# A decoder layer on one core: gathers and chunk loads change rooms, and the order of the sparse steps and of the gates' parts changes

## Chip, cores and metric

The kernel runs on one core of a Trainium2 chip. The time is what one execution takes on the device, in microseconds; each kernel is timed in several executions and the median is given. Engines are called as in the profile: PE (TensorE), DVE (VectorE), ACT (ScalarE), POOL (GpSimd) and SP (SyncE, which issues the large loads). POOL issues the gathers.

## The reference, cut to what matters

The layer has an attention and retention half and a feed-forward half that looks up experts by product keys. The change lies in the second half alone:

```python
PEER_HEADS, PEER_N_KEYS, PEER_TOPK = 8, 128, 16          # 16384 experts, D_MODEL = 2048, SEQ = 256

def peer_ffn(h, w_q, sub_keys, w_u, w_v):
    q = (hf @ w_q).reshape(T, PEER_HEADS, 2, PEER_QUERY_DIM // 2)
    s_half = jnp.einsum('thpd,hpkd->thpk', q, sub_keys)
    v_half, i_half = lax.top_k(s_half, K)
    ...
    top_s, pick = lax.top_k(cand_s, K)
    experts = jnp.take_along_axis(cand_i, pick, axis=-1)
    gates = jax.nn.softmax(top_s, axis=-1)
    ...
        a = jnp.einsum('cd,ced->ce', hc, w_u[ec])
        coef = gc * jax.nn.gelu(a)
        return jnp.einsum('ce,ced->cd', coef, w_v[ec])
```

Each of 256 tokens picks 16 experts in each of 8 heads, with a gate from a softmax over the 16. The result is the gated sum of the experts' v rows, each weighed with gelu of the token's product with the expert's u row. The sum is added to x with a gate and normalised once more.

## The kernel before

**Two ways through the experts.** For the first 192 tokens (`TD`) the kernel computes with all experts: it streams all of u and v, 128 chunks of 1 MB each, and masks by one-hot groups. For the last 64 tokens (`NS`) it gathers rows. The stream runs in four stages of 64 chunks (`HALF`), which fill the span from about 700 us on: `u_half` 0, `v_group` 0, `u_half` 1, `v_group` 1.

- `u_block` takes one u chunk: matmuls for 160 tokens (`TU`) into a PSUM block `psU`, ACT reads it through gelu into `X` (or into `ge`, which DVE multiplies into `X` where the mask is already there). There are two PSUM blocks.
- `v_group` takes one v chunk: ACT casts it to `whi`, DVE subtracts to `wlo` (`split`), ACT and DVE do the same for the coefficients (`cc`), and PE accumulates into eight PSUM banks `acc`: 12 matmuls with `whi`, 8 with `wlo`.
- `g_group` (160 tokens) and `m_group` (the 32 tokens from 160 to 191) make one-hot factors of indices and gates; `g_apply` multiplies them on PE (`pg`) and puts the mask into X. For the 32 tokens the products with u come not from the stream but from gathered rows.

**Sparse steps.** `plan` is a list of 160 steps. Each gathers 128 rows of 8 KB (1 MB) by an indirect DMA of POOL (`gather`) and then does one DVE instruction on them: 32 `m` steps (dots of the 32 tokens, L837, with `h2m`), 64 `u` steps (dots of the 64 tokens, L837, with `h2t`), 64 `v` steps (a chain that adds weighed v rows into `sp`, L843). When the last `m` step is done, `m_done` makes the weights `wm` that the four `m_group`s need; v_group 0 needs their columns of X. `sparse` is called once per chunk; `STEPS` says at which chunks of a stage a step is taken, and in v_group 1 the remaining steps are spread over the chunks. `fetch` keeps up to `most` gathers ahead of the steps.

**Rooms.** `places` says which tile a gather gets. In the u stages it is one of three rooms of `whi`; in v_group 0 one of two rooms of `more`; in v_group 1 a half of `x2` (in the trace `xT`, whose content is no longer needed). The chunk loads take their rooms in turn from the tags that `set_ring` names, always five rooms `raw`, and in the u stages `wlo` and `more` beside them.

**What sets the order.** The program is laid down in the order of the Python code, and a scheduler then fixes one static order of instructions for each engine by its own estimate of times. At run time every engine takes its instructions in that order, and waits where a room or an operand isn't ready.

**Gates.** While u_half 0 runs, a list `work` makes candidates, picks and gates for the two tiles of tokens, and then the groups; an item is taken when enough `budget` (2.4 per block) has gathered. `gates` is one item: DVE subtracts the maximum (`gt`), ACT takes Exp, DVE normalises, PE transposes, ACT casts the gates (`gat`), and for the second tile index and gate rows are copied to the sparse steps' tables.

## Time and profile before

| | us |
|---|---|
| median of 3 executions | 1982.16 (1979.97 to 1984.76) |
| profiled execution, its own time | 1989.1 |
| its span | 1987.3 |
| PE busy | 1825.5 (92%) |
| DVE busy | 1479.9 (74%) |
| ACT busy | 692.9 (35%) |
| POOL busy | 347.4 (17%) |

The stages end at about 1000.5, 1336.7, 1629.1 and 1931.5 us. How to read it: with PE at 92%, what is left lies in the places where PE waits. The slices of the page and stretches of 50 us show where; the timeline then gives the instruction that PE waited for, and what that one waited for. An engine's row stands in its static order, so an instruction that waits holds up all that stands behind it on its engine.

### The profile page before, as it was taken

The page shows a single profiled execution, that of the slowest core. Times are in us where ns is not written, and L with a number is a line of the kernel's source. Part 1 is how long each engine was busy: PE and PEld are TensorE (multiplying, and loading weights), DVE is VectorE, ACT ScalarE, POOL GpSimd, SP SyncE. Part 2 cuts the span into 40 slices and gives each one's busy share as a digit, 9 for nine tenths or more (in the row PEclk, how much of TensorE's full clock was granted, in tenths as well). Part 3 has the DMA queues.
Part 4 walks back from the last instruction along what each step waited for, and adds up shares of the span by engine and source line. Part 5 has one row for each costly group of instructions (what it writes and reads, how often), then busy time and mean ns, then how long its engine had stood idle before and what let it go on. Part 6 is the DMA issues. An engine that isn't in the chain of part 4 may idle for free.

```text
span 1987.3 us, 28481 instructions
## 1 busy us (share of the span) xinstructions
PE 1825.5 (92%) x11302; PEld 1594.7 (80%) x11302; DVE 1479.9 (74%) x2228; ACT 692.9 (35%) x1192; POOL 347.4 (17%) x254
## 2 busy tenths in 40 slices
PE   5798999999969998999939999999999989999982
PEld 4798888898757898999937777779999987777760
DVE  7877888989875795587578878874445658787776
ACT  3344453635343321011024555541111125555531
POOL 1000001021010011211133323221101122323220
PEclk9999999999979999999959999999999999999996
DMA  8989888989974579998978999989999898999963
GB/s 344 371 307 348 344 262 330 337 309 372 365 238 156 174 269 397 407 383 321 364 308 329 369 351 336 345 322 426 393 345 355 330 391 327 363 350 342 347 249 147
DMA packets 94313, 651.86 MB, mean 328 GB/s; under 512 B 11410, under 2 KB 11586, under 8 KB 18402
## 3 DMA queue, kind: packets, MB, share of 16 engines
q1 hardware_dynamic: 66818, 467.78, 62.8%
q0 software_dynamic: 27360, 182.26, 23.6%
q8 instruction: 89, 1.46, 0.3%
q14 instruction: 46, 0.37, 0.1%
HBM read 643.92 MB, written 4.21 MB: 326 GB/s over the span
## 4 chain that ended last, share of the span: by engine, by line
PE 63%; issue 14%; DVE 10%; DMA 9%; ACT 2%; POOL 2%; SPq 0%; POOLq 0%; ACTq 0%; DVEq 0%
PE acc L954 28%; PE psU L1052 17%; PE psN L449 4%; PE psA L235 3%; DMA raw<-in_adaT 3%; DVE wlo L157 2%; DVE raw L197 2%; PE psD L350 2%; PE psA L236 2%; POOL raw L796 1%; PE bkC L350 1%; DMA raw<-in_winA 1%; DMA xT<-in_v,sx 1%; PE bkB L350 1%; ACT whi L156 1%
## 5 line engine op out<-in xcount | busy, mean ns | idle before, releaser
L157 DVE TENSOR_TENSOR wlo<-raw,whi 128x2048 fp32r<-128x2048 f32 (+2 forms) x215 | 481.0, 2239 | 157.6 <-issue 86.8
L1052 PE MATMUL psU<-xT,raw 128*128 128x160 f32 x4096 | 571.1, 301 | 6.0 <-ACT X L1054 6.0
L1052 PEld LDWEIGHTS psU<-xT,raw 128*128 128x128 f32 x4096 | 560.2, 191 | 6.4 <-ACT X L1054 6.3
L156 ACT CAST whi<-raw 128x2048 fp32r<-128x2048 f32 (+2 forms) x215 | 401.7, 1870 | 253.0 <-PE psA L235 40.8
L954 PE MATMUL acc<-whi,cc 128*128 128x512 f32 x1512 | 372.5, 394 | 12.0 <-ACT whi L156 7.3
L954 PEld LDWEIGHTS acc<-whi,cc 128*128 128x128 f32 x1512 | 286.8, 190 | 82.4 <-ACT whi L156 7.6
L954 PE MATMUL acc<-wlo,cc 128*128 128x512 f32 x1008 | 253.8, 392 | 2.3 <-DVE wlo L157 2.3
L197 DVE SCALAR_TENSOR_TENSOR raw<-raw,crow 128x2048 f32<-128x2048 f32 x96 | 219.2, 2285 | 16.7 <-DMA raw<-in_adaT 16.6
L954 PEld LDWEIGHTS acc<-wlo,cc 128*128 128x128 f32 x1008 | 163.0, 162 | 63.6 <-DVE wlo L157 3.1
L449 PE MATMUL psN<-whi,act 128*128 128x512 f32 x512 | 166.8, 401 | 2.2 <-ACT sg L628 1.7
L1054 ACT ACTIVATE X<-psU 128x160 f32<-128x160 f32 (+19 forms) x112 | 28.5, 255 | 384.4 <-PE psU L1052 384.4
L1058 DVE TENSOR_TENSOR X<-X,ge 128x160 f32<-128x160 f32 (+19 forms) x91 | 24.0, 264 | 176.0 <-ACT ge L1057 175.7
L796 POOL DMA_INDIRECT rows<-in_urow,sx x39 | 98.1, 2516 | 210.3 <-DVE rows L837 131.2
L796 POOL DMA_INDIRECT xT<-in_v,sx x38 | 89.8, 2364 | 218.4 <-DVE sp L843 151.5
L930 ACT CAST cc<-X 128x192 fp32r<-128x192 f32 x128 | 44.7, 353 | 220.5 <-PE acc L954 220.2
L449 PEld LDWEIGHTS psN<-whi,act 128*128 128x128 f32 x512 | 96.3, 189 | 25.2 <-ACT sg L628 2.1
L449 PE MATMUL psN<-wlo,act 128*128 128x512 f32 x256 | 103.7, 405 | 6.4 <-DVE wlo L157 6.4
L837 DVE SCALAR_TENSOR_TENSOR raw<-raw,h2m 128x2048 f32<-128x2048 f32 x32 | 73.0, 2287 | 37.4 <-DMA raw<-in_urow,sm__4923 37.4
L843 DVE SCALAR_TENSOR_TENSOR sp<-xT,dots,sp 128x2048 f32<-128x2048 f32 x38 | 89.2, 2347 | 12.4 <-DMA xT<-in_v,sx 12.4
L837 DVE SCALAR_TENSOR_TENSOR rows<-rows,h2t 128x2048 f32<-128x2048 f32 x39 | 89.2, 2287 | 11.2 <-DMA rows<-in_urow,sx 11.2
L235 PE MATMUL psA<-act,whi 128*128 128x512 f32 x240 | 87.5, 406 | 7.6 <-ACT whi L156 7.6
L350 PE MATMUL psD<-act,whi 128*128 128x256 f32 x384 | 76.2, 297 | 3.0 <-ACT whi L156 3.0
(330 smaller groups left out, 2267.1 us busy)
## 6 DMA issues: line engine op xcount, KB each, us to landing
raw<-in_u SPq DMA_DIRECT2D x128, 1024.0 KB, 8.2
raw<-in_v SPq DMA_DIRECT2D x128, 1024.0 KB, 8.5
raw<-in_adaT SPq DMA_DIRECT2D x96, 1024.0 KB, 7.0
raw<-in_winN SPq DMA_DIRECT2D x16, 1024.0 KB, 6.3
raw<-in_woutN SPq DMA_DIRECT2D x16, 1024.0 KB, 7.5
raw<-in_wqT SPq DMA_DIRECT2D x16, 1024.0 KB, 5.8
raw<-in_winB SPq DMA_DIRECT2D x16, 832.0 KB, 6.1
raw<-in_winD SPq DMA_DIRECT2D x12, 1024.0 KB, 6.5
```

Source lines behind the costliest of these rows:

```text
L156: nc.scalar.copy(hi[:, sl], r[:, sl])
L157: nc.vector.tensor_sub(lo[:, sl], r[:, sl], hi[:, sl].bitcast(F32))
L197: nc.vector.scalar_tensor_tensor(r, r, 1.0, crow, op0=OP.mult, op1=OP.mult, accum_out=modc[:, j, k:k + 1])
L235: nc.tensor.matmul(p_, hi[:, sl], act[:, k], start=k == 0, stop=False, skip_group_check=True)
L350: nc.tensor.matmul(bank[:, b, :], x[:, w], y[:, k, :], start=k == k0 and n == 0 and first, stop=k == k1 - 1 and n == 2, skip_group_check=True)
L449: nc.tensor.matmul(ps[tt], x[:, k, ts_], y[:, w], start=k == 0 and j == 0, stop=k == KB - 1 and j == 2)
L796: nc.gpsimd.indirect_dma_start(out=r, out_offset=None, in_=src, in_offset=bass.IndirectOffsetOnAxis(ap=o, axis=0))
L837: nc.vector.scalar_tensor_tensor(r, r, 1.0, h, op0=OP.mult, op1=OP.mult, accum_out=d[:, e:e + 1])
L843: nc.vector.scalar_tensor_tensor(sp, r, dots[:, e:e + 1], sp, op0=OP.mult, op1=OP.add)
L930: nc.scalar.copy(ch, xb(j))
L954: nc.tensor.matmul(acc[c][0:m], x, w[:, c[1] * 512:(c[1] + 1) * 512], start=jj == 0 and n == 0, stop=jj == HALF - 1 and n == 2 - c[0], ski ...
L1052: nc.tensor.matmul(ps, w[:, k * P:(k + 1) * P], xT[:, k, 0:TU], start=k == 0, stop=k == KB - 1)
```

## The change

In words, by part:

1. `STEPS`: u_half 0 takes 41 steps from chunk 14 on (before 40, from 16 on), u_half 1 takes 44 (before 42).
2. `plan` has the 32 `m` steps first, then `u`, then `v` (before `mmmmu` in turn). `m_done` follows step `("u", 1)`.
3. Gathers in the u stages go into `wlo` rooms, each third one into a `more` room (`third_room`); the chunks take `raw` and three `whi` rooms. From chunk 54 on gathers take `more` alone, two at most.
4. v_group 1 takes gathers in halves of `x2` and rooms of `more` in turn, three at most until chunk 30; the steps are spread so that they end four chunks earlier; loads and sums of the end come two to three chunks earlier.
5. `gates` becomes four items: `gates`, `gates_exp`, `gates_turned` (which copies both transposes out of PSUM on ACT) and `gates_by_slots`; the `gat` cast is DVE's. While they are being made the budget per block is 3.3.

The diff, cut:

```diff
-STEPS = dict(u0=[j for j in range(16, HALF - 5) if j not in (17, 31, 45)], v0=[j for j in range(HALF) if j % 8 not in (2, 4, 7)],
-             u1=[j for j in range(HALF - 6) if j % 7 not in (2, 5)])
+STEPS = dict(u0=[j for j in range(14, HALF) if j % 6 != 2], v0=[j for j in range(HALF) if j % 8 not in (2, 4, 7)],
+             u1=[j for j in range(HALF - 2) if j % 7 not in (2, 5)])
...
-        plan = [(k, None) for k in "mmmmu" * (NM // 4) + "u" * (NS - NM // 4) + "v" * NS]
+        plan = [(k, None) for k in "m" * NM + "u" * NS + "v" * NS]
...
-                if (k, e) == ("m", NM - 1):
+                if (k, e) == ("u", 1):
                     m_done()
...
+        def third_room():
+            turn3[0] += 1
+            return more_room() if turn3[0] % 3 == 0 else chunk_tile("raw", F32, "wlo")
+        def more_room():
+            return late.tile([P, D], F32, name="rows", tag="more", bufs=2)
...
+            def either():
+                both[0] += 1
+                return half_of_x2() if both[0] % 2 else more_room()
             if hf:
-                places[0] = half_of_x2
-                set_ring(late, raw=5, more=2)
-            else:
-                places[0] = lambda: late.tile([P, D], F32, name="rows", tag="more", bufs=2)
-                set_ring(late, raw=5)
-            most[0] = 2
-            fetch()
+                places[0], most[0] = either, 3
+                fetch()
...
-                        if j == 24:
-                            set_ring(late, raw=5)
-                        elif j == 34:
+                        if j == 30:
+                            places[0], most[0] = half_of_x2, 2
+                        elif j == 36:
                             g2, gf = fin()
...
-                        elif j == 53:
+                        elif j == 49:
                             most[0] = 1
-                        elif j in (57, 58):
-                            t = j - 57
+                        elif j in (54, 55):
+                            t = j - 54
                             nc.gpsimd.dma_start(z[:, t, :], x2d[:, t, :])
...
-                        elif j == 60:
+                        elif j == 58:
                             nc.vector.tensor_add(z[:, 0, :], z[:, 0, :], s2[:, 0, :])
...
-                        sparse(left[0] / max(1, 56 - j))
+                        sparse(left[0] / max(1, 52 - j))
...
+        def gates_exp(tt):
+            gt = st["gt"]
             nc.scalar.activation(gt, gt, AF.Exp)
...
-            pt = up.tile([P, 2, P], F32, name="ptr", tag=bank("S"))
-            nc.tensor.transpose(pt[:, 0, :], ex.rearrange("p h k -> p (h k)"), ident)
-            nc.tensor.transpose(pt[:, 1, :], gt.rearrange("p h k -> p (h k)"), ident)
+        def gates_turned(tt):
+            ps = up.tile([P, 2, P], F32, name="ptr", tag=bank("S"))
+            nc.tensor.transpose(ps[:, 0, :], flat(st["ex"]), ident)
+            nc.tensor.transpose(ps[:, 1, :], flat(st["gt"]), ident)
+            pt = st["pt"] = tk.tile([P, 2, P], F32, name="pt")
+            nc.scalar.copy(pt, ps)
+        def gates_by_slots(tt):
...
-            nc.scalar.copy(gat[:, 0, ts_], twice(pt[:, 1, 0:nt]))
+            nc.vector.tensor_copy(gat[:, 0, ts_], twice(pt[:, 1, 0:nt]))
...
-            work.append((2.5, lambda j, tt=tt: gates(tt)))
+            work += [(c, lambda j, tt=tt, f=f: f(tt)) for c, f in ((1.5, gates), (2.4, gates_exp), (2.4, gates_turned),
+                                                                   (2.5, gates_by_slots))]
...
-                credit += budget
+                credit += budget if hf or len(work) <= 13 + TD // 8 + 1 else 3.3
...
-                    places[0], most[0] = lambda: chunk_tile("raw", F32, "whi"), 3
+                    places[0], most[0] = third_room, 3
                     if hf:
                         fetch()
-                    set_ring(late, raw=5, wlo=2)
-                if j == 10:
-                    set_ring(late, raw=5, more=1 + hf, wlo=2)
-                if j == HALF - 8:
-                    set_ring(late, raw=5, more=1 + hf)
-                if hf and j == STEPS["u1"][-3]:
-                    most[0] = 1
+                    set_ring(late, raw=5, whi=3)
+                if j == HALF - 10:
+                    places[0], most[0] = more_room, 2
+                if j == HALF - 3:
+                    set_ring(late, raw=5)
```

What this does to the static order is shown at three places. Behind L876 line numbers are 10 higher in the changed kernel, and in the gates some 30. The name before the arrow is what is written, behind it what is read.

First ACT in u_half 0, around the Exp of the second pass of the gates, before:

```order
L1054 ACTIVATE X_5916<-psU 128x160
L807 COPY h2m<-psh 32x512
L1054 ACTIVATE X_5916<-psU 128x160 x9
L1158 CAST gat<-ptr 128x64
L1138 ACT_TABLE_LOAD
L1138 ACTIVATE gt<-gt 128x128
L1054 ACT_TABLE_LOAD
L1054 ACTIVATE X_5916<-psU 128x160 x7
```

and now:

```order
L1064 ACTIVATE X_5916<-psU 128x160
L807 COPY h2m<-psh 32x512
L1064 ACTIVATE X_5916<-psU 128x160 x6
L1184 COPY pt<-ptr 128x256
L1170 ACT_TABLE_LOAD
L1170 ACTIVATE gt<-gt 128x128
L1064 ACT_TABLE_LOAD
L1064 ACTIVATE X_5916<-psU 128x160 x10
```

Exp (`gt<-gt`) stood behind nine reads of X that follow the last `h2m` copy, and stands behind six.

Second DVE at the end of u_half 0, around the weights of the 32 tokens (`dotm`, `wmT`, `wm`; `o2m` are their one-hot groups), before, down to the first of them behind the last product X:

```order
L1058 TENSOR_TENSOR X_6925<-X_6925,ge 128x160 x2
L837 SCALAR_TENSOR_TENSOR raw,dotm<-raw,h2m 128x2048
L1058 TENSOR_TENSOR X_6925<-X_6925,ge 128x160
L837 SCALAR_TENSOR_TENSOR raw,dotm<-raw,h2m 128x2048
L1058 TENSOR_TENSOR X_6925<-X_6925,ge 128x160 x2
L837 SCALAR_TENSOR_TENSOR raw,dotm<-raw,h2m 128x2048 x2
L814 TENSOR_TENSOR dotm<-dotm,sm__4923 128x32
L837 SCALAR_TENSOR_TENSOR rows,dots<-rows,h2t 128x2048
L815 STREAM_TRANSPOSE wmT<-dotm 128x32
L817 CAST wm<-wmT 128x64
L819 TENSOR_TENSOR wmT<-wmT,wm 128x32
L1027 TENSOR_TENSOR o2m<-eqm,wm 128x512
```

and now:

```order
L1068 TENSOR_TENSOR X_6929<-X_6929,ge 128x160
L837 SCALAR_TENSOR_TENSOR raw,dotm<-raw,h2m 128x2048
L1068 TENSOR_TENSOR X_6929<-X_6929,ge 128x160
L814 TENSOR_TENSOR dotm<-dotm,sm__4923 128x32
L815 STREAM_TRANSPOSE wmT<-dotm 128x32
L817 CAST wm<-wmT 128x64
L819 TENSOR_TENSOR wmT<-wmT,wm 128x32
L1037 TENSOR_TENSOR o2m<-eqm,wm 128x512
L817 CAST wm<-wmT 128x64
L819 TENSOR_TENSOR wmT<-wmT,wm 128x32
L1037 TENSOR_TENSOR o2m<-eqm,wm 128x512
```

The weights stood behind all products of the stage's X, and stand ahead of the last six.

Third DVE between u_half 1 and v_group 1 (`sp<-...` are v steps; `raw` are `wlo` rooms now and `whi` rooms before, `rows` are rooms of `more`), before:

```order
L843 SCALAR_TENSOR_TENSOR sp<-raw,dots,sp 128x2048
L1058 TENSOR_TENSOR X_6925<-X_6925,ge 128x160
L843 SCALAR_TENSOR_TENSOR sp<-raw,dots,sp 128x2048
L1058 TENSOR_TENSOR X_6925<-X_6925,ge 128x160 x2
L843 SCALAR_TENSOR_TENSOR sp<-raw,dots,sp 128x2048 x3
L157 TENSOR_TENSOR wlo<-raw,whi 128x2048 x3
L931 TENSOR_TENSOR cc<-X_5916,cc 128x192
L157 TENSOR_TENSOR wlo<-raw,whi 128x2048
L931 TENSOR_TENSOR cc<-X_5916,cc 128x192
```

and now, from the fourth step behind the last product X on:

```order
L843 SCALAR_TENSOR_TENSOR sp<-raw,dots,sp 128x2048 x2
L843 SCALAR_TENSOR_TENSOR sp<-rows,dots,sp 128x2048
L843 SCALAR_TENSOR_TENSOR sp<-raw,dots,sp 128x2048 x2
L843 SCALAR_TENSOR_TENSOR sp<-rows,dots,sp 128x2048
L843 SCALAR_TENSOR_TENSOR sp<-raw,dots,sp 128x2048 x2
L843 SCALAR_TENSOR_TENSOR sp<-rows,dots,sp 128x2048
L843 SCALAR_TENSOR_TENSOR sp<-raw,dots,sp 128x2048 x2
L843 SCALAR_TENSOR_TENSOR sp<-rows,dots,sp 128x2048
L843 SCALAR_TENSOR_TENSOR sp<-raw,dots,sp 128x2048
L157 TENSOR_TENSOR wlo<-raw,whi 128x2048
L843 SCALAR_TENSOR_TENSOR sp<-raw,dots,sp 128x2048
```

Behind the last product X three v steps stood ahead of the first `wlo`, and sixteen stand there now, three above these rows and thirteen in them. On POOL the two gathers into `xT`, which wait for PE's end of u_half 1, stood behind all but one of the stage's gathers into `raw`, and stand ahead of the fourth of these sixteen.

## Rows read from the trace of the kernel before

**Rows 1.** the stretches: start:end, length, busy PE, PEld, DVE, ACT, POOL (instructions), PEclk, DMA, GB/s

```profile
750.00:800.00 50.00, 43.99 (x309) 43.75 (x308) 32.40 (x44) 5.71 (x13) 8.95 (x9) 0.93 0.98 396
...
1600.00:1650.00 50.00, 42.67 (x318) 39.31 (x317) 31.48 (x30) 14.52 (x28) 9.48 (x8) 0.90 1.00 412
```

**Rows 2.** the timeline in u_half 0 (start, us, engine, line, op [idle before <-releaser])

```profile
752.70 0.30 ACT L1054 ACTIVATE X<-psU 128x160 f32<-128x160 f32 x1 [4.04 <-PE psU L1052]
...
768.63 2.29 DVE L837 SCALAR_TENSOR_TENSOR raw<-raw,h2m 128x2048 f32<-128x2048 f32 x1 [2.59 <-DMA raw<-in_urow,sm__4923]
...
773.77 2.29 DVE L837 SCALAR_TENSOR_TENSOR raw<-raw,h2m 128x2048 f32<-128x2048 f32 x1 [2.84 <-DMA raw<-in_urow,sm__4923]
...
777.01 0.28 DVE L1137 TENSOR_TENSOR gt<-tv 128x128 f32<-128x128 f32 x1
...
777.36 1.28 ACT L1138 ACT_TABLE_LOAD   x1
...
780.63 9.56 PE L1052 MATMUL psU<-xT,raw 128*128 128x160 f32 x53 [6.01 <-ACT X L1054]
```

**Rows 3.** the timeline from u_half 0 to v_group 0, DVE and PE

```profile
965.81 2.28 DVE L837 SCALAR_TENSOR_TENSOR raw<-raw,h2m 128x2048 f32<-128x2048 f32 x1
...
994.73 5.73 PE L1052 MATMUL psU<-xT,raw 128*128 128x160 f32 x41
...
1003.29 2.29 DVE L837 SCALAR_TENSOR_TENSOR raw<-raw,h2m 128x2048 f32<-128x2048 f32 x1
...
1009.32 0.21 PE L1037 MATMUL pg<-o2m,o1m 128*128 128x64 bf16 x1 [8.86 <-DVE o2m L1027]
...
1031.82 0.45 PE L1037 MATMUL pg<-o2m,o1m 128*128 128x64 bf16 x2 [6.19 <-DVE o2m L1027]
```

**Rows 4.** the timeline from u_half 1 to v_group 1, POOL, DVE and PE

```profile
1623.64 0.94 POOL L796 DMA_INDIRECT raw<-in_v,sx  x1 [1.95 <-DVE sp L843]
...
1629.31 0.94 POOL L796 DMA_INDIRECT xT<-in_v,sx  x1 [1.24 <-PE psU L1052]
...
1629.65 4.73 DVE L843 SCALAR_TENSOR_TENSOR sp<-raw,dots,sp 128x2048 f32<-128x2048 f32 x2
...
1635.57 2.35 DVE L843 SCALAR_TENSOR_TENSOR sp<-raw,dots,sp 128x2048 f32<-128x2048 f32 x1 [1.19 <-DMA raw<-in_v,sx]
...
1636.37 5.46 PE L954 MATMUL acc<-whi,cc 128*128 128x512 f32 x12 [7.33 <-ACT whi L156]
...
1643.50 2.00 PE L954 MATMUL acc<-whi,cc 128*128 128x512 f32 x8
```

**Rows 5.** the timeline of the tail, PE, POOL and DVE

```profile
1927.39 4.09 PE L954 MATMUL acc<-pair,cc 128*64 128x512 f32 x17
...
1941.09 0.93 POOL L796 DMA_INDIRECT xT<-in_v,sx  x1 [4.53 <-DVE sp L843]
...
1946.88 2.35 DVE L843 SCALAR_TENSOR_TENSOR sp<-xT,dots,sp 128x2048 f32<-128x2048 f32 x1 [3.21 <-DMA xT<-in_v,sx]
...
1952.03 2.04 PE L980 MATMUL pc<-sp,sel 128*128 128x512 f32 x2 [20.55 <-DVE sp L843]
...
1966.08 0.69 DVE L982 TENSOR_TENSOR tg<-pc,g 128x512 f32<-128x512 f32 x1 [1.68 <-PE pc L981]
...
1969.51 0.69 DVE L982 TENSOR_TENSOR tg<-pc,g 128x512 f32<-128x512 f32 x1
```

**Rows 6.** the chain that ended last, v_group 0 and u_half 1 (start, us, what)

```profile
1096.21 240.53 PE acc L954 x1052
...
1615.22 0.70 PE pg L1037 x24
...
1615.92 13.14 PE psU L1052 x96
```

**Rows 7.** the timeline of v_group 1, DVE, one chunk with an sp step

```profile
1850.56 0.35 DVE L931 TENSOR_TENSOR cc<-X,cc 128x192 fp32r<-128x192 f32 x1
...
1855.29 0.35 DVE L931 TENSOR_TENSOR cc<-X,cc 128x192 fp32r<-128x192 f32 x1
```

More of the change, by code (lines that the diff above doesn't have):

```diff
@@ L884, in half_of_x2 @@
                 return x2[:, turn_[0] % 2, :]
+            def either():
+                both[0] += 1
+                return half_of_x2() if both[0] % 2 else more_room()
+            both = [0]
             if hf:
-                places[0] = half_of_x2
-                set_ring(late, raw=5, more=2)
-            else:
-                places[0] = lambda: late.tile([P, D], F32, name="rows", tag="more", bufs=2)
-                set_ring(late, raw=5)
-            most[0] = 2
-            fetch()
+                places[0], most[0] = either, 3
+                fetch()
             with tc.tile_pool(name=f"vsb{hf}", bufs=1) as vb:
@@ L1132, in pick, with rows_of @@
             nc.vector.reduce_sum(st["ex"][:, h, :], ei, axis=AX.X)
+        def rows_of(i, x):
+            nc.gpsimd.dma_start(sx[0:NS, i, :], x[NS:P, 0:NS])
+            nc.vector.tensor_copy(sx[NS:P, i, :], x[NS:P, NS:P])
+            for qd in range(4):
+                dst, src = sm_[qd * NM:(qd + 1) * NM, i, :], x[TU - P:TD - P, qd * NM:(qd + 1) * NM]
+                if qd * NM == TU - P:
+                    nc.vector.tensor_copy(dst, src)
+                else:
+                    nc.gpsimd.dma_start(dst, src)
+        flat = lambda x: x.rearrange("p h k -> p (h k)")
         def gates(tt):
             tv, ex = st["tv"], st["ex"]
-            gt = tk.tile([P, 8, 16], F32, name="gt")
+            if tt == 1:
+                rows_of(0, flat(ex))
+            gt = st["gt"] = tk.tile([P, 8, 16], F32, name="gt")
             nc.vector.tensor_sub(gt, tv, tv[:, :, 0:1].to_broadcast([P, 8, 16]))
+            if tt == 1:
+                nc.vector.tensor_copy(off, sx[:, 0, :])
+                nc.vector.tensor_copy(offm, sm_[:, 0, :])
+        def gates_exp(tt):
+            gt = st["gt"]
             nc.scalar.activation(gt, gt, AF.Exp)
@@ L1143, in gates @@
             nc.vector.tensor_mul(gt, gt, sm[:, :, None].to_broadcast([P, 8, 16]))
[L1144 to L1146 removed]
+            if tt == 1:
+                rows_of(1, flat(gt))
+        def gates_turned(tt):
[5 more added lines that the diff above has]
+        def gates_by_slots(tt):
+            pt = st["pt"]
             nt = P if tt == 0 else NS
@@ L1206, in u_half @@
                 u_block(pool, hf, j, groups[0])
-                credit += budget
+                credit += budget if hf or len(work) <= 13 + TD // 8 + 1 else 3.3
                 while work and (credit >= work[0][0] or j == HALF - 1):
-                    if not hf and len(work) <= NM // 8 + 1 and plan.index(("m", NM - 1)) > len(plan) - left[0] - 1:
+                    if not hf and len(work) <= NM // 8 + 1 and plan.index(("u", 1)) > len(plan) - left[0] - 1:
                         break
```

16 lines of the change are left out of this document (1 added, 15 removed).

## The prediction

> **What bounds the kernel now.** The page's first part comes first: TensorE (PE) is busy 1825.5 of 1987.3 us, VectorE (DVE) 1479.9. So an edit pays only where PE stands idle, and the stretches of 50 us say where that is. From 650 us on nearly all are full; [rows 1] are two that are not. The timeline and the chain of waits, read around each hole, give four with a cause that the change touches.
>
> (a) In u_half 0 PE waits 6.01 us until 780.63 for X, ScalarE's read of a PSUM block [rows 2]. ScalarE is held up by its Exp, which waits for DVE's subtraction `gt` (777.01), and that stands behind four dots whose gathered rows arrive one by one (DVE waits 2.59 and 2.84 us ahead of the last two).
>
> (b) Between u_half 0 and v_group 0 PE waits for the groups of the 32 tokens (`o2m`): five waits, the first 8.86 us, the last 6.19 [rows 3], 25.7 us together. The last of their 32 dots starts at 1003.29, after the last u matmul (994.73 + 5.73 = 1000.46).
>
> (c) Between u_half 1 and v_group 1 three `sp` steps stand on DVE ahead of the first `wlo`; PE idles 7.33 us and starts cold [rows 4].
>
> (d) Behind the last accumulation `sp` steps and their gathers remain: PE waits 20.55 us for the last of them [rows 5].
>
> **The sum's base.** All terms are set against the profiled execution (span 1987.3, its own time 1989.1). The runs' median, 1982.16, lies 6.9 below that; I put the difference found in the span on the median.
>
> **Gates (a).** Four pieces cost nothing in count: one copy of both transposes on ScalarE replaces the cast there, and the `gat` cast goes to DVE, which is busy 32.4 of 50 us there [rows 1]. The order matters more. Exp now stands behind the X of block 11 (read at 752.70), three X earlier, and DVE's subtraction behind three dots where it stood behind four. The first gathers are released by the same steps as before, so I take the same arrivals. The third dot ends at 768.63 + 2.29 = 770.9. Before, gt began 0.95 after the fourth dot's end (773.77 + 2.29), and PE went on 3.62 after gt: now at 775.5, or 1.28 earlier where ScalarE loads its activation table (777.36) while it waits. PE runs two blocks past the last X read, each a third of 13.14 us [rows 6]: to 761.5. The stall is 12.7 to 14.0 instead of 6.0 us. I take **+6.5**; if the three arrivals come closer together it can shrink to +2; upward +8.
>
> **32 tokens first (b).** With m dots first in the plan all 32 are among the first 32 steps; the chain behind them follows u step 1, the 34th. By the order, these groups lie inside the last u blocks on DVE and PE, and PE goes from the last u matmul to the first accumulation. Could the gathers hold that up? Before, the 34th dot of any kind ran at 965.81 [rows 3], 34.6 us ahead of the end of u_half 0, so the data were there in time under the same load. The hole's size: v_group 0 runs from 1000.46 to 1336.74 = 336.3 us. Its undisturbed part ran 1052 matmuls in 240.53 us [rows 6], 0.2286 each; 64 chunks of 20 need 292.7. So 43.6 are lost. What stays: four groups of about 0.70 us [rows 6], now inside u_half 0 (2.8), and some 3.8 for the first chunk's cast and the first waits for `wlo`. 43.6 - 6.6: **-37** (-39.5 to -30).
>
> **Rooms and what they queue (c).** The largest term, and a loss. In the u stages gathers now use `wlo` rooms and every third time one of `more`; `wlo` rooms are what v_group 1 needs first. The v rows take two of them early, while the last u dots go one by one through `more`, so the steps fall behind: by the order, DVE has done 104 steps at the last X product, 118 before, and then there are **sixteen** sp in a row ahead of the first wlo, where three stood. PE's first twelve matmuls need no wlo; then it waits. T0 is the end of u_half 1 (1615.92 + 13.14 = 1629.06 before). The sixteen start at T0 + 0.6, as 1629.65 did. Three have their rows; they end at T0 + 7.7 (4.73 for two). The fourth gather stands on POOL behind the two xT gathers, which wait for PE's end (1629.31 did so), and is issued at about T0 + 3.3, when the first sp has freed a room. How long does it take? With PE stopped, the five `raw` rooms fill and chunk loads cease; so the nearest row is not the loaded one (issued 1623.64, sp at 1635.57: 11.9 us) but the tail's (issued 1941.09, sp at 1946.88: 5.8 us, two in flight). With three in flight here I add a transfer of 2.5 us (1 MB at 412 GB/s, [rows 1]): the fourth sp starts at T0 + 11.4. From there a room's cycle is 0.3 issue + 5.6 landing + 2.35 sp = 8.25 us, and three sp pass in each: 2.75 apiece. The fourth and twelve more, 11.4 + 2.35 + 12 x 2.75 = 46.75, and wlo 2.2: T0 + 49. Then chunk 1 waits for two more sp and its own wlo (7 us, of which PE works 4.7) and ends at T0 + 49 + 7 + 1.8, where 9.1 were ideal: a loss of 48.7, with a cold start (1.0) 49.7. Before, chunk 0 ended at 1643.50, 14.4 after T0, 4.6 of it work: loss 9.8. **+40**. If DVE alone sets the pace, wlo ends at 0.6 + 16 x 2.36 + 2.2 = 40.6, so +31. If a sp takes 3.05 and the fourth starts at T0 + 15: +47.
>
> The Trainium skill (DMA: Bandwidth & Descriptors, Anatomy of one DMA) fits one GpSimd-issued transfer by 2.0 us plus the bytes over 436 kB per us, 4.4 us for 1 MB. The tail's 5.8 us disagrees, and the measurement decides; by the page the cycle would be 7.05, an estimate, and this term about 5 smaller.
>
> **v_group 1 after that.** By the order some twelve chunks carry one sp each, where one in two did. With wlo and sp DVE takes 1855.29 - 1850.56 = 4.73 us from `cc` to `cc` [rows 7], against 20 x 0.2286 = 4.57 on PE: 0.16 x 12 = 2, and 0.5 for a late gather: **+2.5** (1 to 6). That is two MB per chunk, some 450 GB/s, above the 412 of [rows 1]; the five full rooms cover 5 MB of it, which is why I take no more.
>
> **The tail (d).** All sp now stand ahead of the last pair's wlo, z loads and their addition too. The end of acc (1927.39 + 4.09 = 1931.5) is then followed by pc. What comes behind tg stays: 1987.3 - 1969.51 = 17.8. From the first pc to that tg 17.5 us passed (1952.03 to 1969.51) with a cold start; warm it is 2.1 for pc and three steps of 3.43 (1966.08 to 1969.51), 12.4. I take 13.5. So the end comes 31.3 behind acc, before 55.8: **-24.5** (-26 to -21).
>
> **Sum**: 6.5 - 37 + 40 + 2.5 - 24.5 = -12.5. Median 1982.16 - 12.5 = **1970**. The term of the queue carries most of the doubt.
>
> **Rivals.**
> - *The queue runs at the loaded latency* (slower). If chunk loads go on beside it, a cycle is 0.3 + 11.9 + 2.35 = 14.55, 4.85 per sp: 12 x 2.1 = 25 more, and the fourth starts 3.6 later: +28.6, sum +16, **1998**. The sign turns where a sp costs 1.04 more (12.5 over twelve), a landing of about 9 us. For it: DMA share 1.00 in 1600 to 1650; against it: the tail's rows. Chance 0.14.
> - *DVE alone paces the queue*: sum -21.5, **1961**. For it: four rooms, where the tail has two; against it: the tail's sp waits 3.21 us for its rows. 0.20. The Trainium skill's fit, above, points this way.
> - *The chain of the 32 tokens still comes late* (slower): its gathers slip six blocks, 26 us, and the 25.7 us come back: +13, **1995**. For it: DMA share 0.98 in 750 to 800 and dots that wait; against: 965.81. 0.08.
> - *The change doesn't do in the tail what it says*: gathers come late, sp steps remain ahead of pc or hold up wlo; half of the 24.5 is lost: sum 0, **1982**. 0.08.
>
> **How the numbers follow.** My forecast has 0.50. A measurement can tell 0.2%, 4 us, so faster is below 1978.2 and slower above 1986.1. Of the forecast 0.05 falls within; faster is 0.45 + 0.20 and 0.08 of cases in which the first or third rival comes in small part or the tail's loss meets a short queue: 0.73; within 0.12; slower 0.15. The range, 1953 (DVE's pace, good bounds elsewhere) to 1988, leaves out the two late cases at their full price.
>
> **What would show it.** In the trace after: sixteen sp between the last X product and the first wlo, PE idle some 40 us there, and the time from issue to sp, 5.6 or 12; no wait for o2m behind 1000; one X wait of 12 to 14 us from 762 on; pc at once behind acc, and the end 31 us behind it. Wrong would be: PE stalls inside u_half 1 (DVE waiting for a dot in `more` while three X are due), or chunk loads running on beside the queue.

## The result, and the profile after

| | before | after |
|---|---|---|
| median of 16 executions, us | 1990.11 (1979.97 to 1994.67) | 1979.93 (1969.95 to 1983.73) |
| span of the profiled execution, us | 1987.3 | 1979.1 |

The ratio after to before is 0.995, with a 95% interval of 0.9934 to 0.9966: the changed kernel is half a per cent faster, 10 us. The three runs shown ahead of the prediction had 1982.16; over sixteen the same kernel has 8 us more, and the lowest of the sixteen is one of the three.

The page of the changed kernel, part 1 and one row of the 40 slices:

```profile
PE 1815.2 (92%) x11302; PEld 1588.4 (80%) x11302; DVE 1481.0 (75%) x2231; ACT 693.7 (35%) x1188; POOL 352.9 (18%) x254
...
PE   5799999999969998999999999999999916999995
```

The gap at slice 21 is closed, a wider one stands at slice 33 (it reads 1), and the last slices are fuller. Divided at the points that the prediction used, the two profiled executions differ so (us):

| stretch | before | after | difference | forecast |
|---|---|---|---|---|
| until the first X of u_half 0 | 703.2 | 700.8 | -2.4 | 0 (same order; scatter) |
| u_half 0, to its last u matmul | 297.2 | 299.6 | +2.3 | +9.3 (gates 6.5, groups 2.8) |
| from there to the end of u_half 1 | 628.6 | 585.9 | -42.7 | -39.8 |
| from there to the end of acc | 302.4 | 363.0 | +60.6 | +42.5 (queue 40, chunks 2.5) |
| behind acc | 55.8 | 29.8 | -26.0 | -24.5 |
| sum | 1987.3 | 1979.1 | -8.2 | -12.5 |

The first stretch has the same instructions in the same order in every kernel of this document, and took 699.5 to 710.5 us in their fourteen profiles. So single spans that differ by some us tell nothing; stretches behind that point, and waits, can be compared.

PE's waits from 690 us on (what was waited for: us in total, times, longest):

```profile
PE acc L964 <- DVE wlo L157: 66.2, 3, 62.1
PE psU L1062 <- ACT X L1064: 6.3, 1, 6.3
PE pc L990 <- DVE te L988: 4.4, 3, 1.5
PE acc L964 <- DVE cc L941: 1.0, 1, 1.0
```

No wait for `o2m` and none of `pc` for `sp` is left. They answer to [rows 3] and [rows 5]. One wait of 62.1 us for `wlo` has taken their place.

**Gates.** The timeline (start, us, engine, line, operation, idle before) answers to [rows 2]:

```profile
750.28 0.30 ACT L1064 ACTIVATE X<-psU 128x160 f32<-128x160 f32 x1 [4.04 <-PE psU L1062]
...
750.64 2.29 DVE L837 SCALAR_TENSOR_TENSOR raw<-raw,h2m 128x2048 f32<-128x2048 f32 x1 [6.34 <-ACT X L1064]
...
760.03 2.29 DVE L837 SCALAR_TENSOR_TENSOR rows<-rows,h2m 128x2048 f32<-128x2048 f32 x1 [2.56 <-DMA rows<-in_urow,sm__4923]
...
763.15 0.28 DVE L1163 TENSOR_TENSOR gt<-tv 128x128 f32<-128x128 f32 x1
...
765.44 16.82 PE L1062 MATMUL psU<-xT,raw 128*128 128x160 f32 x101 [6.28 <-ACT X L1064]
```

Block 11's X is read at 750.28, Exp stands behind it as the order said, and PE waits 6.28 us. The first row's dot starts 0.4 us after that X; before it was 6.3 us (752.70 to 759.02).

**Into v_group 0**, PE's timeline, against [rows 3]:

```profile
997.95 2.42 PE L1062 MATMUL psU<-xT,raw 128*128 128x160 f32 x16
1000.10 1.21 PE L964 MATMUL acc<-whi,cc 128*128 128x512 f32 x4
1002.30 1.19 PE L964 MATMUL acc<-whi,cc 128*128 128x512 f32 x4 [0.99 <-DVE cc L941]
```

PE goes from the last u matmul to the first `acc` without a gap and waits once, 0.99 us.

**Into v_group 1**, PE, DVE and POOL, against [rows 4]:

```profile
1585.96 3.05 PE L964 MATMUL acc<-whi,cc 128*128 128x512 f32 x12
...
1586.85 2.35 DVE L843 SCALAR_TENSOR_TENSOR sp<-raw,dots,sp 128x2048 f32<-128x2048 f32 x1
...
1591.55 0.94 POOL L796 DMA_INDIRECT raw<-in_v,sx  x1 [0.30 <-issue]
...
1594.60 2.35 DVE L843 SCALAR_TENSOR_TENSOR sp<-raw,dots,sp 128x2048 f32<-128x2048 f32 x1 [5.41 <-DMA raw<-in_v,sx]
...
1597.22 2.93 POOL L796 DMA_INDIRECT raw<-in_v,sx  x1 [4.73 <-DVE sp L843]
...
1604.47 2.35 DVE L843 SCALAR_TENSOR_TENSOR sp<-raw,dots,sp 128x2048 f32<-128x2048 f32 x1 [5.13 <-DMA raw<-in_v,sx]
...
1607.10 0.94 POOL L796 DMA_INDIRECT raw<-in_v,sx  x1 [5.70 <-DMA raw<-in_v,sx]
...
1607.14 2.35 DVE L843 SCALAR_TENSOR_TENSOR sp<-raw,dots,sp 128x2048 f32<-128x2048 f32 x1 [0.31 <-DMA raw<-in_v,sx]
...
1646.36 2.35 DVE L843 SCALAR_TENSOR_TENSOR sp<-raw,dots,sp 128x2048 f32<-128x2048 f32 x1 [1.61 <-DMA raw<-in_v,sx]
...
1648.75 2.29 DVE L157 TENSOR_TENSOR wlo<-raw,whi 128x2048 fp32r<-128x2048 f32 x1
...
1651.10 3.78 PE L964 MATMUL acc<-wlo,cc 128*128 128x512 f32 x8 [62.08 <-DVE wlo L157]
```

u_half 1 ends at 1586.24 (T0). Twelve `acc` matmuls follow, then PE waits. On DVE the first queued step has its row, the second waits 5.41 us for it, the fourth starts at 1604.47 (T0 + 18.2), the sixteenth at 1646.36 (41.9 us for twelve, 3.49 each), and the first `wlo` ends at T0 + 64.8. The row of the fourth step is issued at 1591.55 and used 12.9 us later; the next, issued at 1597.22, is used at 1607.14, 9.9 us later; behind that the rows that DVE waits for take 6.8 to 10.1 us. What the DMA engines moved from 1595 to 1600 (in all; then the gathers' queue: packets, MB, share of the engines):

```profile
DMA packets 294, 2.13 MB, mean 426 GB/s; under 512 B 34, under 2 KB 34, under 8 KB 34
...
q0 software_dynamic: 292, 2.13, 100.8%
```

The next two windows of 50 us (columns as in [rows 1]) show what the DMA engines did there, and later beside the chunks:

```profile
1600.00:1650.00 50.00, 0.00 (x0) 0.00 (x0) 31.82 (x14) 0.00 (x0) 21.71 (x14) 0.50 0.81 299
1700.00:1750.00 50.00, 50.00 (x221) 38.75 (x220) 47.86 (x32) 23.83 (x34) 22.78 (x9) 1.00 1.01 423
```

In 1600 to 1650 PE is idle at a granted clock of 0.50, which is 1.2 of 2.4 GHz, and comes back cold: eight matmuls take 3.78 us, where eight warm ones take 1.99. The 299 GB/s are 15 MB, which is what fourteen gathers carry: the chunk loads had ceased, as forecast, but not at once. From T0 to 1595 they still moved 1.46 MB beside 2.02 MB of gathers. Behind that gathers ran alone, and still took longer than the 5.6 us forecast.

**Behind acc**, PE and DVE, against [rows 5]:

```profile
1945.17 4.10 PE L964 MATMUL acc<-pair,cc 128*128 128x512 f32 x17
...
1949.11 1.02 PE L990 MATMUL pc<-sp,sel 128*128 128x512 f32 x2
...
1961.30 0.69 DVE L992 TENSOR_TENSOR tg<-pc,g 128x512 f32<-128x512 f32 x1
```

`pc` follows acc at once, warm; the fourth `tg` comes 12.2 us behind the first `pc` (17.5 before).

### The profile page after: what moved, and what is told of

It is laid out like the page before. It is cut to its first block, busy times and chain, and to the rows that moved or that the text cites. A ratio compares the mean times of both kernels' runs of the same rounds, so it can differ in the third digit from the quotient of the medians.

```text
span 1979.1 us, 28429 instructions
## 1 busy us (share of the span) xinstructions
PE 1815.2 (92%) x11302; PEld 1588.4 (80%) x11302; DVE 1481.0 (75%) x2231; ACT 693.7 (35%) x1188; POOL 352.9 (18%) x254
## 3 DMA queue, kind: packets, MB, share of 16 engines
q8 instruction: 89, 1.46, 0.3%
## 4 chain that ended last, share of the span: by engine, by line
PE 57%; issue 19%; DMA 11%; DVE 8%; POOL 2%; ACT 2%; SPq 0%; POOLq 0%; ACTq 0%; DVEq 0%
PE acc L964 27%; PE psU L1062 11%; PE psA L235 3%; PE psN L449 3%; DMA raw<-in_v,sx 3%; DMA raw<-in_adaT 2%; DVE wlo L157 2%; PE bkB L350 2%; DVE raw L197 2%; PE psA L236 2%; PE psD L350 2%; DMA rows<-in_v,sx 1%; POOL rows L796 1%; DMA raw<-in_winA 1%; PE bkC L350 1%
## 5 line engine op out<-in xcount | busy, mean ns | idle before, releaser
L964 PE MATMUL acc<-wlo,cc 128*128 128x512 f32 x1008 | 255.7, 394 | 66.2 <-DVE wlo L157 66.2
L796 POOL DMA_INDIRECT rows<-in_urow,sx x53 | 104.7, 1976 | 392.5 <-DVE rows L837 364.3
L837 DVE SCALAR_TENSOR_TENSOR rows<-rows,h2t 128x2048 f32<-128x2048 f32 x53 | 121.1, 2286 | 3.4 <-DMA rows<-in_urow,sx 3.4
L796 POOL DMA_INDIRECT xT<-in_v,sx x24 | 60.6, 2524 | 128.2 <-DVE sp L843 75.7
L350 PE MATMUL bkA<-act,whi 128*128 128x256 f32 x256 | 53.7, 307 | 17.0 <-DVE act L295 13.4
L236 PE MATMUL psA<-act,wlo 128*128 128x256 f32 x240 | 68.6, 287 | 0.5 <-DVE wlo L157 0.5
```

Source lines behind the costliest of these rows:

```text
L236: nc.tensor.matmul(p_[:, 1, :], lo[:, sl], hh[:, k, :], start=False, stop=k == KB - 1, skip_group_check=True)
L350: nc.tensor.matmul(bank[:, b, :], x[:, w], y[:, k, :], start=k == k0 and n == 0 and first, stop=k == k1 - 1 and n == 2, skip_group_check=True)
L796: nc.gpsimd.indirect_dma_start(out=r, out_offset=None, in_=src, in_offset=bass.IndirectOffsetOnAxis(ap=o, axis=0))
L837: nc.vector.scalar_tensor_tensor(r, r, 1.0, h, op0=OP.mult, op1=OP.mult, accum_out=d[:, e:e + 1])
L964: nc.tensor.matmul(acc[c][0:m], x, w[:, c[1] * 512:(c[1] + 1) * 512], start=jj == 0 and n == 0, stop=jj == HALF - 1 and n == 2 - c[0], ski ...
```

## The experiments

All ratios are against the kernel before, with runs of both on the same chip. "Into v_group 0" and "into v_group 1" give PE's longest wait at that change of stage in us, and for what (before: 8.9 for o2m and 7.3 for whi); "behind acc" is the time from the end of acc to the end of the span. Two further kernels, short_sp and no_ring_10, ran once each and are told of by their rows alone.

| run | what it is | ratio (95%) | into v_group 0 | into v_group 1 | behind acc |
|---|---|---|---|---|---|
| m_first | before + m steps first | 0.9943 (0.9922 to 0.9965) | 14.8, whi | 24.0, whi | 44.0 |
| v1_rooms | before + v_group 1's part | 0.9877 (0.9846 to 0.9908) | 8.9, o2m | 7.3, whi | 32.4 |
| u_rooms | before + u stages' rooms | 1.0073 (1.0045 to 1.0101) | 13.2, o2m | 18.2, wlo | 61.2 |
| rooms_back | after, rooms of before | 0.9865 (0.984 to 0.989) | 20.8, whi | 26.4, whi | 29.9 |
| more_at_54 | rooms_back, more from 54 | 0.9916 (0.9894 to 0.9938) | none, but loads late | none | 29.8 |
| gates_back | after, gates of before | 0.9947 (0.9918 to 0.9976) | none | 53.2, wlo | 29.8 |
| v0_half | after, 32 steps in v_group 0 | 0.9885 (0.9852 to 0.9918) | none | 30.8, wlo | 49.3 |
| balanced | v0_half, v_group 1 longer | 0.9838 (0.9797 to 0.9879) | none | 32.8, wlo | 35.5 |
| m_first_v1 | before + m first + v_group 1 | 0.9827 (0.9783 to 0.9871) | 15.1, whi | 23.8, whi | 29.9 |
| queue_to_tail | balanced, more from 44 | 0.9868 (0.984 to 0.9896) | none | 5.7, wlo | 68.3 |

### One part of the change alone

The 32 m steps first, nothing else:

```diff
-        plan = [(k, None) for k in "mmmmu" * (NM // 4) + "u" * (NS - NM // 4) + "v" * NS]
+        plan = [(k, None) for k in "m" * NM + "u" * NS + "v" * NS]
...
-                if (k, e) == ("m", NM - 1):
+                if (k, e) == ("u", 1):
...
```

> Only the plan is changed: the 32 m steps first, the weights behind u step 1; rooms, gates and v_group 1 as before. Theory (holes close one by one, and a queue of sp ahead of the first wlo costs some 3.7 us per sp, as in the changed kernel's trace): PE has no wait for o2m, -40 us; by the order six sp stand ahead of the first wlo where three stood, +11; five are left behind the last wlo instead of eight, some -8: about 37 us less than before, ratio 0.981. Rival (the steps only move; what the first hole gives back is paid behind u_half 1 by the dots that v_group 0 must now do beside its chunks): the queue takes back most, ratio 0.990 to 1.00.

The rival came out. PE's waits in it, and ACT's first cast of v_group 0:

```profile
PE acc L954 <- ACT whi L156: 38.8, 2, 24.0
...
1014.48 1.90 ACT L156 CAST whi<-raw 128x2048 fp32r<-128x2048 f32 x1 [12.54 <-DVE raw L837]
```

`o2m` is gone from the list, but a wait for `whi` stands at both changes of stage, 14.8 and 24.0 us. Gathers lie in `whi` rooms, dots that have come late use them up, and only then can ACT cast the next stage's first chunk (it waits 12.54 us for a dot, L837). v_group 0 is 26.3 us shorter than before (310.0 against 336.3) and v_group 1 21.9 longer (324.3 against 302.4). So the order of the plan alone doesn't close the first hole; I had put the whole -37 on it.

Only v_group 1's part:

```diff
-                places[0] = half_of_x2
-                set_ring(late, raw=5, more=2)
+                places[0], most[0] = either, 3
...
-                        sparse(left[0] / max(1, 56 - j))
+                        sparse(left[0] / max(1, 52 - j))
...
```

> Only v_group 1 is changed: gathers in halves of x2 and rooms of more in turn, three at most, steps spread to chunk 52, z loads and sums earlier. Theory: the tail alone shrinks. Two sp stay behind the last wlo where eight stood; the end lies some 36 us behind the last accumulation instead of 56: 20 us less, ratio 0.990; three sp ahead of the first wlo as before. Rival (three gathers in flight beside the chunk loads are what makes v_group 1 60 us longer in the changed kernel): v_group 1 grows by 20 us or more, ratio 1.00 or above.

```profile
PE acc L961 <- ACT whi L156: 7.3, 1, 7.3
```

As the theory said: the wait into v_group 1 is the 7.3 us of before, v_group 1's accumulation takes 295.4 us (295.1 before), and the part behind it 32.4 instead of 55.8. Three gathers at a time don't slow the chunks here. This part alone is 1.2% faster than before, more than the whole change.

Only the rooms of the u stages:

```diff
-                    places[0], most[0] = lambda: chunk_tile("raw", F32, "whi"), 3
+                    places[0], most[0] = third_room, 3
...
-                    set_ring(late, raw=5, wlo=2)
+                    set_ring(late, raw=5, whi=3)
...
+                if j == HALF - 10:
+                    places[0], most[0] = more_room, 2
...
```

> Only the rooms of the u stages are changed: gathers in wlo rooms and every third in more, chunks in raw and three whi rooms, more alone from chunk 54. Theory: by the order six sp stand ahead of the first wlo where three stood, in wlo rooms, and nine instead of eight behind the last wlo: PE idles some 20 us there instead of 7, +13 to +18 in all, ratio 1.007 to 1.009. Rival (the queue of sixteen is the room swap's own work): sixteen in a row as in the changed kernel, +50, ratio 1.025.

```profile
PE pc L989 <- DVE sp L843: 27.5, 1, 27.5
PE acc L963 <- DVE wlo L157: 22.1, 6, 18.2
```

Six sp stand in the queue, and the longest wait is 18.2 us. The room swap alone makes a short queue, not sixteen.

### The changed kernel with one part undone

```diff
-                    places[0], most[0] = third_room, 3
+                    places[0], most[0] = lambda: chunk_tile("raw", F32, "whi"), 3
...
-                    set_ring(late, raw=5, whi=3)
+                    set_ring(late, raw=5, wlo=2)
...
```

> The changed kernel with the rooms of the u stages as before (gathers in three whi rooms, chunks in raw, wlo and more); plan, gates, steps and v_group 1 stay changed. Theory: by the order seven sp stand ahead of the first wlo instead of sixteen and none behind the last: PE's wait of 62 us falls to some 25, first hole and tail stay closed: 45 to 55 us less than before, ratio 0.973 to 0.977. Rival (the queue comes from the m steps being first or from v_group 1's three rooms, not from the u stages' rooms): PE still idles over 50 us there, ratio 0.99 to 0.995.

PE's timeline at the two changes of stage:

```profile
1021.31 4.21 PE L967 MATMUL acc<-whi,cc 128*128 128x512 f32 x9 [20.81 <-ACT whi L156]
...
1636.62 3.65 PE L967 MATMUL acc<-whi,cc 128*128 128x512 f32 x8 [26.36 <-ACT whi L156]
```

The second wait is the 25 us of the theory, but the first hole opens again by 20.8 us, for `whi`, so its total didn't come. With m_first and u_rooms this shows what closes the hole in the changed kernel: m steps first and the changed rooms of the u stages, both together; neither does it alone.

That asks for gathers in `whi` rooms until chunk 54 and in `more` behind that (beside the edit of rooms_back):

```diff
+                if j == HALF - 10:
+                    places[0], most[0] = more_room, 2
+                    set_ring(late, raw=5)
...
```

> The changed kernel with gathers of the u stages back in the three whi rooms until chunk 54, and then in rooms of more, two at most, so that no whi or wlo room is held by a gather when a v stage begins. Theory (what costs is a queue of steps that hold the rooms which the next stage casts into): by the order no step stands between the last X product and the first wlo at either change of stage, and none behind the last wlo. Neither o2m nor whi nor wlo keep PE waiting over 3 us there, the end lies 30 us behind acc: 43 + 10 + 26 us less than before, and some 5 of that given back: 70 to 78, ratio 0.961 to 0.965. Rival (the dots that the first hole hid must be paid somewhere: the steps' own DVE time and gathers fill the chunks and slow them): chunks in v_group 1 take 4.8 instead of 4.57, or PE waits for wlo all along, ratio 0.97 to 0.98.

PE's waits, and then SP's own queue from 940 to 1060:

```profile
PE psU L1065 <- DMA raw<-in_u: 54.3, 3, 37.1
...
PE acc L967 <- DVE wlo L157: 1.9, 1, 1.9
```

```profile
SPq L147 <- DVE rows L837: 37.5, 1, 37.5
```

No v stage waits at its start, but PE waits 54.3 us in the u stages for chunk loads. In this version loads still take rooms of `more` in turn, and a load behind a gather whose step is not done (37.5 us in one case) holds all loads behind it on SP. The changed kernel had taken `more` out of the loads' ring; my version left that out until chunk 54 and again from 56 on, and it can't tell whether the steps fit.

Gates in one piece:

```diff
-            work += [(c, lambda j, tt=tt, f=f: f(tt)) for c, f in ((1.5, gates), (2.4, gates_exp), (2.4, gates_turned),
-                                                                   (2.5, gates_by_slots))]
+            work.append((2.5, lambda j, tt=tt: gates(tt)))
...
```

> The changed kernel with the gates in one piece as before, and their budget. By the order thirteen sp stand ahead of the first wlo instead of sixteen, worth some 11 us. For the X wait in u_half 0, which I had priced +6.5 for the change: theory (the order alone decides, but the first rows land some 8 us sooner in the changed kernel since its chunk loads are further ahead): Exp stands three X later again, so PE waits 0 to 2 us for X instead of 6.3. Rival (arrivals follow the gates' order, nothing else): 6.0 as in the kernel before. Together 11 to 17 us less than the changed kernel, ratio 0.986 to 0.989 against the kernel before.

```profile
PE acc L964 <- DVE wlo L157: 56.4, 4, 53.2
PE psU L1062 <- ACT X L1064: 5.9, 1, 5.9
PE pg L1047 <- DVE o L1020: 4.8, 2, 4.6
```

The X wait is 5.9 us against 6.3, so the four pieces gain or lose nothing in that wait. The rival's 6.0 came out, but not for its reason: the rows come as early as in the changed kernel (7.1 us after issue), and in this order five dots stand ahead of `gt`. The queue is shorter by three sp and its wait by 8.9 us. Against that u_half 0 takes 6.2 us more (305.8 against 299.6), with 4.8 us of waits for `o`, the groups of the 160 tokens, and the ratio is that of the changed kernel, which neither theory nor rival had.

### What a queued step costs

Fewer steps asked in v_group 0:

```diff
-v0=[j for j in range(HALF) if j % 8 not in (2, 4, 7)]
+v0=[j for j in range(HALF) if j % 2 == 0]
```

> The changed kernel with 32 steps asked in v_group 0 instead of 40. By the order the same 105 steps are done at the end of u_half 1, but seven sp stand ahead of the first wlo instead of sixteen, and six behind the last one instead of none. Theory (the queue is what was asked and couldn't be done; each queued sp costs 3.7 us): PE's wait for wlo falls from 62 to some 29 us, the tail grows by some 14 to 20: 13 to 19 us less than the changed kernel, ratio 0.985 to 0.989. Rival (the wait belongs to the change of stage, by the xT gathers that wait for PE, not to the number of steps): it stays over 50 us, ratio 1.00.

```profile
PE acc L964 <- DVE wlo L157: 33.5, 3, 30.8
```

Theory held: seven sp in the queue, 30.8 us; and 19.5 us more behind acc (49.3). The queue's length sets the wait. With 13 sp (gates_back) the wait is 53.2, with 16 it is 62.1: from 7 to 16 it grows by 31.3, 3.48 per step.

Each v step over 512 columns:

```diff
-                    nc.vector.scalar_tensor_tensor(sp, r, dots[:, e:e + 1], sp, op0=OP.mult, op1=OP.add)
+                    nc.vector.scalar_tensor_tensor(sp[:, 0:512], r[:, 0:512], dots[:, e:e + 1], sp[:, 0:512], op0=OP.mult, op1=OP.add)
```

> The changed kernel with each v step cut to 512 of its 2048 columns (three quarters of the weighed sum are left out); gathers as they are, and the order with sixteen steps ahead of the first wlo too. In the changed kernel three of these steps take 10 to 12.7 us. Theory (a gather that is issued while the next step runs on DVE spends 2.93 us on POOL instead of 0.94, and the rest of its landing is its own): a step takes 0.6 us, POOL's long ones vanish, and three steps take 0.3 + 5.2 + 0.6 = 6 to 7 us; the wait for wlo falls from 62 to some 35. Rival (the transfers themselves set the pace, three in flight share what the DMA engines give): landing stays at 7 to 10 us and three steps take 8 to 11 us; the wait falls to no less than 45.

DVE and POOL in the queue:

```profile
1603.18 0.75 DVE L843 SCALAR_TENSOR_TENSOR sp<-raw,dots,sp 128x512 f32<-128x512 f32 x1 [12.62 <-DMA raw<-in_v,sx]
...
1604.20 0.94 POOL L796 DMA_INDIRECT raw<-in_v,sx  x1 [11.13 <-DVE sp L843]
...
1610.83 0.75 DVE L843 SCALAR_TENSOR_TENSOR sp<-raw,dots,sp 128x512 f32<-128x512 f32 x1 [3.66 <-DMA raw<-in_v,sx]
...
1636.41 0.75 DVE L843 SCALAR_TENSOR_TENSOR sp<-raw,dots,sp 128x512 f32<-128x512 f32 x1 [3.62 <-DMA raw<-in_v,sx]
```

From 1603.18 to 1636.41 twelve steps pass, 8.3 us for three; a row issued at 1604.20 is used at 1610.83, 6.6 us later, and the later ones that DVE waits for take 6.6 to 8.3 us. PE's wait is 49.3 us. That is the rival: the transfers set most of the pace. Work on DVE fell by 3 x 1.6 = 4.8 us for three steps, the time for three by 10.5 - 8.3 = 2.2. No run varies how many transfers are in flight in the queue itself; the tail of queue_to_tail, below, has two.

### The first rows

The kernel before, without one room for the loads:

```diff
-                if j == 10:
-                    set_ring(late, raw=5, more=1 + hf, wlo=2)
```

> The kernel before without the chunk loads' extra room of more from chunk 10 on. It is a look at the first gathered rows of u_half 0. Counted from ACT's read of block 11 they were issued 4.6 to 5.8 us ahead and landed after 9.7 to 11.0 us in all kernels with the rooms of before, and 6.9 to 7.1 ahead and after 7.1 to 7.5 us in all with the changed rooms. Theory (chunk 10 is when those are issued, and there the loads get one more room and fetch ahead into it): without it they land after 7 to 8 us. Rival (it is the whi or wlo rooms, or how far the loads have come by then): 9.7 us or more, as before. For the span: five sp ahead of the first wlo of v_group 1 where three stood, six behind the last where eight stood; about the same, 1975 to 1990 us.

POOL's first gather, the first dot, and PE's wait:

```profile
747.01 1.06 POOL L796 DMA_INDIRECT raw<-in_urow,sm__4923  x1 [4.20 <-DVE sm__4923 L1174]
...
754.29 2.29 DVE L837 SCALAR_TENSOR_TENSOR raw<-raw,h2m 128x2048 f32<-128x2048 f32 x1 [6.12 <-DMA raw<-in_urow,sm__4923]
...
780.38 4.90 PE L1052 MATMUL psU<-xT,raw 128*128 128x160 f32 x17 [4.46 <-ACT X L1054]
```

Issued 747.01, used at 754.29: 7.3 us, as in every kernel with the changed rooms (7.1 to 7.5). It is issued 7.0 us ahead of ACT's read of block 11 (754.00), before 4.6 us ahead. So the late rows of the kernel before came from an extra room that the loads were given at chunk 10, when those gathers were issued. The execution took 1980.36 us, within the 1975 to 1990 expected; `gt` still stands behind four dots, and PE's wait for X falls only to 4.46 us.

### Where the rest of the steps can go

```diff
-                        if j == 30:
+                        if j == 42:
                             places[0], most[0] = half_of_x2, 2
...
-                        sparse(left[0] / max(1, 52 - j))
+                        sparse(left[0] / max(1, 57 - j))
...
```

(beside v0_half's line; the loads and sums of the end come three to ten chunks later)

> The changed kernel with the steps spread anew: 32 asked in v_group 0 instead of 40, and v_group 1 keeps its three gather rooms until chunk 42 (30), takes steps up to chunk 57 (52) and loads and sums for the end later. By the order seven sp stand ahead of the first wlo instead of sixteen, and three behind the last one. Theory (some 105 steps fit beside the stream until the end of u_half 1, whatever is asked; each step asked beyond that costs 3.5 us in the queue, each left at the end about as much): the wait for wlo is 31 us as with seven in the run before, the tail 37 to 42 us instead of 30: some 20 us less than the changed kernel, ratio 0.982 to 0.986. Rival (v_group 1 can't carry more steps: three gathers at a time beside its chunks make PE wait for wlo chunk by chunk): v_group 1's part after the queue grows from 298 to over 305 us, ratio 0.990 or above.

```profile
PE acc L964 <- DVE wlo L157: 34.5, 2, 32.8
```

As expected, 1954.39 us: v_group 1 carries 45 steps beside its chunks, and behind acc 35.5 us are left.

The kernel before with m steps first and this v_group 1:

> The kernel before with two parts of the change, the 32 m steps first and v_group 1's three gather rooms (kept until chunk 42, steps up to 57); the rooms of the u stages, the gates and the steps asked are as before. By the order five dots stand ahead of the first wlo of v_group 0, six sp ahead of that of v_group 1, none behind the last. Theory (gathers in whi rooms hold what the next v stage casts into: each change of stage costs a wait for whi of some 15 and 24 us, as with m steps alone; the tail closes): 15 + 24 + 30 where before lost 36 + 7 + 56: some 30 us less, ratio 0.983 to 0.987. Rival (parts gained alone add up: 0.9943 x 0.9877): 0.982 or below, with the waits for whi no longer than m steps alone.

```profile
PE acc L961 <- ACT whi L156: 39.0, 2, 23.8
```

1954.50 us: the waits for `whi` (15.1 and 23.8) are those of m_first, the tail is closed. The ratio lies between the two forecasts, which are too close for its interval to tell apart; the waits are the theory's. Both kernels beat the changed one, and against each other they are the same.

The balanced kernel with the gathers of u_half 1 in `more` alone from chunk 44:

```diff
-                if j == HALF - 10:
+                if j == HALF - (20 if hf else 10):
```

> The balanced kernel with u_half 1's gathers in rooms of more alone from chunk 44 (before it 54). By the order the queue ahead of the first wlo shrinks from seven sp to one, and nine instead of three are left behind the last wlo. Theory (what doesn't fit beside the stream costs about 3.5 us per step wherever it stands): the wait for wlo falls from 33 to 3 to 10 us, the tail grows from 35 to 55 to 60: within 6 us of the balanced kernel, ratio 0.981 to 0.987. Rival (a step in the queue is dearer, since PE also goes cold and the room chain restarts; or cheaper behind the end, where nothing else loads): 10 us or more below the balanced kernel, ratio 0.979 or below.

```profile
PE pc L990 <- DVE sp L843: 35.3, 1, 35.3
PE acc L964 <- DVE wlo L157: 8.3, 2, 5.7
...
1909.14 0.94 POOL L796 DMA_INDIRECT xT<-in_v,sx  x1 [3.26 <-DVE sp L843]
...
1914.64 2.35 DVE L843 SCALAR_TENSOR_TENSOR sp<-xT,dots,sp 128x2048 f32<-128x2048 f32 x1 [1.80 <-DMA xT<-in_v,sx]
```

The queue's wait falls by 27, the part behind acc grows by 33. The ratio lies in the theory's range, and its interval overlaps that of balanced; the rival is refuted. The medians differ by 10 us, but they come from two chips, and of the 10.3 us between the two profiled spans 6.6 lie ahead of u_half 0. v_group 1 and the part behind acc together are 5.5 us longer. So a step at the end is at most a little dearer than one in the queue. The tail itself is longer than the 55 to 60 us expected: two rooms are left, a row takes 5.5 to 5.7 us from issue to use (1909.14 to 1914.64), a step comes each 4.1 us, and the loads of `z` wait for the rooms of the last two.

## Why the prediction came out as it did

**The base.** This step failed first. I put the sum on the median of the three runs shown, although the profiled execution's own time, 1989.1, lay 6.9 above it. Sixteen runs have 1990.11. The sum was -12.5, measured are -10 in the medians and -8.2 in the profiles; on the right base the forecast would have been 1977.6, and 1979.93 was measured. That the sum came so near is luck: against their forecasts the stretches are off by -2.4 (scatter), -7.0, -2.9, +18.1 and -1.5 us, and these cancel to +4.3.

**Gates, +6.5: wrong; measured +0.3** (a wait of 6.28 us against 6.01 in [rows 2]). The order and the stall's mechanism were read rightly (Exp behind block 11, PE two blocks on). "I take the same arrivals" failed. The first rows land after 7.5 instead of 10.9 us and are issued earlier, since the chunk loads no longer take a `more` room at chunk 10; no_ring_10 shows it on the kernel before. The first dot starts 5.9 us earlier after block 11's X (0.4 against 6.3), which is nearly all of the 6.2 us by which the term was too dear. A change of rooms for the loads was in the diff, and I had costed it at nothing.

**32 tokens first, -37: right in size, too short in its reason.** From the last u matmul of u_half 0 to the end of u_half 1 42.7 us are gained, 39.8 were forecast. But m_first, u_rooms and rooms_back show that the plan's order gives it only together with the rooms.

**The queue, +40: mis-sized; with the chunks behind it +60.6 instead of +42.5.** This is the term that failed most. Sixteen steps, twelve matmuls ahead, chunk loads ceased (9 us late): as forecast. Two numbers were not. The fourth step started at T0 + 18.2 instead of 11.4 (6.8 us): three rows were taken as ready and one was; the fourth gather was issued at T0 + 5.3, forecast 3.3, and took 12.9 us, forecast 8.1, behind the `rows` and `xT` gathers issued just ahead of it and beside the last chunk loads (426 GB/s moved from 1595 to 1600). And twelve more steps took 3.49 us each, forecast 2.75 (8.9 us). The 5.6 us for a landing came from a tail with two gathers in flight, and with two it takes 5.5 to 5.7 us in queue_to_tail as well. With three in flight it takes 6.6 to 8.3 us even where DVE does a third of the work (short_sp). The prediction added a transfer of 2.5 us for the fourth row because three were in flight, and left it out of the cycle behind that; with it the cycle would have been 10.75 us, 3.58 per step. Both measured numbers lie beyond the prediction's own bad case (3.05, and T0 + 15). In the changed kernel a gather issued while a step runs costs POOL 2.93 us (1597.22, beside the step from 1596.99), one issued just ahead of a step 0.94 (1607.10); short_sp, where it is 0.94 to 1.33, shows that this isn't what sets the pace. The Trainium skill (SBUF — State Buffer, Who interferes with whom) says that a DVE instruction with two inputs in SBUF contends with GpSimd instructions that read SBUF; sp has two such inputs, a gather reads its row numbers from `sx`, and this trace agrees with its 2.93 and 0.94.

**The first rival** (slower, loaded latency) was right for the start of the queue, where loads still moved: the fourth row took 12.9 us, where it had 11.9. Behind 1595 there were no loads, and its price of 4.85 per step was too high, mine too low. DVE's own pace, 2.35, is refuted. The Trainium skill's fit for one transfer (DMA: Bandwidth & Descriptors, Anatomy of one DMA), an estimate of 4.4 us for 1 MB by the prediction's working, points to that pace too; the landings here, 6.8 to 12.9 us with several in flight, differ from it, and the measurement decides.

**Chunks behind the queue, +2.5.** Two more waits for `wlo`, 0.96 and 3.15 us, and 4.1 us of slower matmuls (363.0 less the three waits, 66.2, against 292.7) stand where the prediction had 5.8 in all; with the queue's 15.7 that makes up the 18.1 missing.

**The tail, -24.5: right**, -26.0. pc and tg ran warm throughout, 12.2 us where 13.5 were taken.

## What to carry to other kernels

A static order pins what was asked for, not what fits: when gathered steps fall behind, they queue ahead of the first instruction that needs their room, and the next stage waits for all of them. Count the steps ahead of each stage's first cast, take gathers out of that stage's rooms some blocks early, and don't let loads on an in-order queue share rooms with gathers whose use is uncertain. A landing time is to be taken from a row with as many transfers in flight as the place will have.
